# A state-space layer whose scan tables come from DRAM and whose states lie on partition halves

## The chip, the cores and the metric

The kernel runs on one core of a Trainium2 chip. The metric is the device time of one execution in microseconds, as a median of timed runs. The engines are TensorE (PE; PEld is its weight load), VectorE (DVE), ScalarE (ACT), GpSimd (POOL) and SyncE (SP); DMA transfers are issued from SP's, ACT's and POOL's queues.

## The reference

One sequence of 512 tokens with 2048 channels, in float32, passes through a state-space (S5) layer and then a forgetting-attention layer. What matters here is the first: 128 groups of 16 channels, each with 64 complex states.

```python
def s5_ssm(u, a_re, a_im, log_dt, b_re, b_im, c_re, c_im, d_skip):
    """u: (B,S,W) -> Re(C h_t) + D*u_t, h_t = Abar h_{t-1} + Bbar u_t per 16-channel group."""
    ...
    x_re = coef_re * bu_re - coef_im * bu_im
    x_im = coef_re * bu_im + coef_im * bu_re
    ...
    _, _, h_re, h_im = lax.associative_scan(combine, (a_seq_re, a_seq_im, x_re, x_im), axis=1)
    y = (jnp.einsum('bsgp,gcp->bsgc', h_re, c_re.astype(F32))
         - jnp.einsum('bsgp,gcp->bsgc', h_im, c_im.astype(F32)))
    y = y + d_skip.astype(F32).reshape(S5_GROUPS, S5_GROUP) * uf
    return y.reshape(bsz, seq, S5_WIDTH)

def s5_layer(h, g_pre, g_post, w_in, ...):
    xn = rmsnorm(h, g_pre)
    uz = xn @ w_in
    u, z = jnp.split(uz, 2, axis=-1)
    y = s5_ssm(u, a_re, a_im, log_dt, b_re, b_im, c_re, c_im, d_skip)
    y = jax.nn.gelu(y)
    y = y * jax.nn.sigmoid(y @ w_glu.astype(F32) + b_glu.astype(F32))
    y = y.astype(h.dtype) * jax.nn.silu(z)
    return h + rmsnorm(y @ w_out, g_post)
```

## The kernel before

All large products are float32 as three products of split halves (`mm3`, L170 to L172): ACT rounds a weight block `wraw` to `whi` (L84), DVE takes the rest as `wlo` (L151). Phase A (0 to 456 us) holds the 32 projections by `w_in`, 16 blocks of 128 channels of u and 16 of z, each 48 matmuls of 128x512, and the state-space layer in 16 tiles j of 128 channels (8 groups; `NQ` is 4 pairs of groups). Phase B multiplies by `w_glu`, C by `w_out`; then comes attention to 1600 us and the last product. `order_a` lists the steps of phase A: after the start, each tile's `tab`, `ker`, `scan` and `y` stand between projections, so that about three projections go with two tiles. A tile scheduler at build time makes each engine's order from it; the weight loads run on POOL's queue through four `wraw` buffers.

A sequence is cut into 64 chunks of `CL` = 8 tokens. `ssm_params` makes the powers of the decay (`apow`, states on partitions: 64 states of two groups). For each tile, `ssm_tables` builds Bt, powers times the input matrix, on DVE (L72, 128x1024, three operations), turns it by eight PE transposes (`btps`, L424) and copies it to BT by ACT; it also makes the phasors `rot`. `ssm_kernel` builds Et, powers times the output matrix (three operations of 128x1152), multiplies it by `bb` to the taps of a chunk (`kps`, L464), from which DVE and ACT make `ktp`; this goes to DRAM (`kd`, L471) and comes back in eight transfers as the Toeplitz matrix M (L475). `ssm_u` turns u by eight writes to DRAM (`ub`, L485) and one read (U, L487), all on SP. `ssm_scan` takes U times BT (`xps`, L498, real and imaginary apart), rotates it, runs the scan G on DVE (L510) and writes the states before each chunk to `hbd`, a block-diagonal tile in which a pair of groups has 128 columns. `ssm_y` adds two products in `yps`: Et times hbd (L526, 8 matmuls of 128x128), and M times U (L531, 16 of 64x64 on alternating column halves). ACT takes the gelu, and eight writes (`y_d`, L537, SP) store it. z goes to DRAM (`z_d`, L700) on ACT's queue.

The profile counts a float32 matmul as two: the 8 of L526 are 16 rows of the trace, the 16 of L531 are 32; a transpose is one.

Of the kernel before, what the change touches and what calls it, by code (L numbers as in the profile page):

```python
# [1153 lines left out]
```

## Time and profile before

| | |
|---|---|
| three timed runs | 1797.41 us median, 1794.77 to 1800.89 |
| the profiled execution | 1793.25 us, span 1791.5 us |
| granted TensorE clock | 0.998 of full speed (its 2.4 GHz level) |
| PE, DVE, ACT, POOL busy | 1772.2, 1100.7, 588.9, 345.3 us |
| phase A, in which the change lies | 0 to 456 us |

A busy share is an average over phases. In a stage in which PE never pauses, an engine of lower share can still be near its limit; what a step costs is read from its own stretch.

### The profile page before, as it was taken

How to read it: one execution, taken by the hardware profiler on the slowest of the kernel's cores; microseconds unless marked ns; L12 is line 12 of the kernel's file. 1: busy time of each engine (PE TensorE's matmuls, PEld its weight loads, DVE VectorE, ACT ScalarE, POOL GpSimd, SP SyncE). 2: the span in 40 equal slices, each digit the busy share in tenths (PEclk: the TensorE clock that was granted, in tenths of full speed). 3: DMA queues.
4: the chain of work that ended last, by engine and by line, in shares of the span. 5: the costliest groups of instructions: out<-in, count | busy, mean ns of one | idle time of the engine just before them, and what ended most of it. 6: DMA issues, size and time to landing. Idle time of an engine off the chain costs nothing.

```text
span 1791.5 us, 24986 instructions
## 1 busy us (share of the span) xinstructions
PE 1772.2 (99%) x9942; PEld 1504.9 (84%) x9942; DVE 1100.7 (61%) x1598; ACT 588.9 (33%) x977; POOL 345.3 (19%) x241
## 2 busy tenths in 40 slices
PE   9999999999999999999999999999999999999997
PEld 6888888888888888898888888888888888988887
DVE  9789899985765622356664666455654556552235
ACT  7333332322544322225332323232332333332221
POOL 1000000000100000012433433334333343300000
PEclk9999999999999999999999999999999999999999
DMA  9545555545644453343333322232233222235332
GB/s 325 152 136 154 142 153 147 150 144 163 213 148 149 160 190 102 98 135 119 95 89 95 90 94 89 93 99 89 89 93 97 91 96 88 89 118 176 98 113 97
DMA packets 141334, 226.49 MB, mean 126 GB/s; under 512 B 53601, under 2 KB 80497, under 8 KB 140961
## 3 DMA queue, kind: packets, MB, share of 16 engines
q1 hardware_dynamic: 126000, 173.79, 31.4%
q0 software_dynamic: 13056, 47.33, 8.3%
q10 hardware_dynamic: 2160, 3.77, 0.6%
q8 instruction: 78, 1.28, 0.3%
q14 instruction: 40, 0.32, 0.1%
HBM read 201.88 MB, written 22.97 MB: 126 GB/s over the span
## 4 chain that ended last, share of the span: by engine, by line
PE 91%; DVE 4%; DMA 2%; SPq 1%; issue 0%; ACT 0%; DVEq 0%; ACTq 0%
PE proj L170 18%; PE proj L172 18%; PE proj L171 18%; PE tok L230 6%; PE tok L231 6%; PE tok L232 6%; PE v L205 3%; PE v L204 3%; PE v L206 3%; PE yps L526 1%; PE t L938 1%; PE yps L531 1%; PE xps L498 1%; DVE al L75 1%; PE btps L424 1%; DVE wlo L151 1%
## 5 line engine op out<-in xcount | busy, mean ns | idle before, releaser
L151 DVE TENSOR_TENSOR wlo<-wraw,whi 128x1024 fp32r<-128x1024 f32 x284 | 421.9, 1487 | 453.5 <-ACT whi L84 453.4
L84 ACT ACTIVATE whi<-wraw 128x1024 fp32r<-128x1024 f32 (+2 forms) x292 | 305.9, 1049 | 848.8 <-PE proj L172 508.2
L147 POOL TENSOR_TENSOR wraw<-wraw,vecs 128x1024 f32<-128x1024 f32 (+1 forms) x128 | 263.0, 2055 | 622.1 <-DMA wraw<-kv_k 254.8
L170 PE MATMUL proj<-BH,whi 128*128 128x512 f32 (+1 forms) x816 | 309.8, 380 | 0.0
L171 PE MATMUL proj<-BH,wlo 128*128 128x512 f32 (+1 forms) x816 | 307.7, 377 | 2.0 <-DVE wlo L151 2.0
L172 PE MATMUL proj<-BL,whi 128*128 128x512 f32 (+1 forms) x816 | 308.0, 377 | 0.5 <-DVE BL L72 0.5
L170 PE MATMUL proj<-ah,whi 128*128 128x512 f32 x768 | 302.2, 394 | 2.1 <-ACT zt L84 1.8
L171 PE MATMUL proj<-ah,wlo 128*128 128x512 f32 x768 | 299.4, 390 | 0.1
L172 PE MATMUL proj<-al,whi 128*128 128x512 f32 x768 | 299.1, 390 | 0.0
L171 PEld LDWEIGHTS proj<-BH,wlo 128*128 128x128 f32 x816 | 153.6, 188 | 30.2 <-DVE wlo L151 2.4
L172 PEld LDWEIGHTS proj<-BL,whi 128*128 128x128 f32 x816 | 153.5, 188 | 29.3 <-DVE BL L72 0.8
L170 PEld LDWEIGHTS proj<-BH,whi 128*128 128x128 f32 x816 | 153.6, 188 | 27.6
L170 PEld LDWEIGHTS proj<-ah,whi 128*128 128x128 f32 x768 | 144.1, 188 | 33.8 <-ACT zt L84 2.2
L171 PEld LDWEIGHTS proj<-ah,wlo 128*128 128x128 f32 x768 | 144.2, 188 | 30.4 <-DVE wlo L151 0.7
L172 PEld LDWEIGHTS proj<-al,whi 128*128 128x128 f32 x768 | 144.2, 188 | 30.3 <-DVE al L75 0.3
L205 PE MATMUL v<-wlo,BH 128*128 128x512 f32 (+2 forms) x320 | 111.4, 348 | 0.0
L204 PE MATMUL v<-whi,BH 128*128 128x512 f32 (+2 forms) x320 | 111.3, 348 | 0.0
L206 PE MATMUL v<-whi,BL 128*128 128x512 f32 (+2 forms) x320 | 111.3, 348 | 0.0
L230 PE MATMUL tok<-whi,BH 128*128 128x512 f32 (+1 forms) x320 | 111.1, 347 | 0.0
L230 PE MATMUL tok<-whi,ah 128*128 128x512 f32 (+1 forms) x320 | 111.0, 347 | 0.0
L232 PE MATMUL tok<-whi,al 128*128 128x512 f32 (+1 forms) x320 | 110.9, 347 | 0.0
L231 PE MATMUL tok<-wlo,ah 128*128 128x512 f32 (+1 forms) x320 | 110.9, 347 | 0.0
(211 smaller groups left out, 2359.9 us busy)
## 6 DMA issues: line engine op xcount, KB each, us to landing
wraw<-w_fox SPq DMA_DIRECT2D x64, 512.0 KB
wraw<-w_in POOLq DMA_DIRECT2D x58, 512.0 KB, 4.3
wraw<-w_glu POOLq DMA_DIRECT2D x32, 512.0 KB, 4.4
wraw<-w_out SPq DMA_DIRECT2D x32, 512.0 KB
wraw<-kv_k SPq DMA_DIRECT2D x32, 512.0 KB
wraw<-w_fo SPq DMA_DIRECT2D x32, 512.0 KB
wraw<-kv_v SPq DMA_DIRECT2D x28, 512.0 KB
M<-kd SPq DMA_DIRECT2D x128, 64.0 KB
```

The costliest lines, as they stand in the source:

```text
L84: self.nc.scalar.activation(out, in_, f, **kw)
L147: (eng or nc.vector).tensor_tensor(raw, raw, scale.unsqueeze(2).to_broadcast(shp), op=ALU.mult)
L151: (eng if eng and scale is None else nc.vector).tensor_tensor(lo, raw, hi, op=ALU.subtract)
L170: mm(ps, lhsT=hi, rhs=xh, start=(k == 0), stop=False)
L171: mm(ps, lhsT=lo, rhs=xh, start=False, stop=False)
L172: mm(ps, lhsT=hi, rhs=xl, start=False, stop=(k == self.K - 1))
L204: nc.tensor.matmul(o, lhsT=xh[k][:, bs], rhs=hi, start=(k == 0), stop=False)
L205: nc.tensor.matmul(o, lhsT=xh[k][:, bs], rhs=lo, start=False, stop=False)
L206: nc.tensor.matmul(o, lhsT=xl[k][:, bs], rhs=hi, start=False, stop=(k == K - 1))
L230: nc.tensor.matmul(ps, lhsT=xh[k][:, bs], rhs=hi, start=(k == 0), stop=False)
L231: nc.tensor.matmul(ps, lhsT=xh[k][:, bs], rhs=lo, start=False, stop=False)
L232: nc.tensor.matmul(ps, lhsT=xl[k][:, bs], rhs=hi, start=False, stop=(k == K - 1))
```

## The change

- The powers are turned on PE once at the start (`ssm_powers`, new L397, 8 transposes `aps`) and B once for four tiles (`ssm_group`, new L425, 4 transposes `bgps`). Both go to DRAM (`at_d`, `bt_d`). For each tile, `ssm_fetch` reads them back spread over partitions (AT, BTab, 512 KB each, one buffer each, on SP), after the tables of the tile before are made; `ssm_tables` multiplies them to BT directly on DVE. The transposes `btps` and ACT's copies of them are gone.
- Real and imaginary states of a group lie on the two partition halves. H is one tile `hst` of 8 groups by 64 chunks, written by four adds of 64x252 in place of two of 64x504 to `hbd`. The E product (new L563) is 16 matmuls of 64x64, on alternating column halves. Et is 128x1024 from DVE, with its first step of 128x128 copied by ACT; it takes `apow2`, the powers by group, which ACT copies at the start in eight pieces of 64x576.
- u is written in one transfer (`ub`, SP) and read in one. The eight `y_d` writes of a tile and z go on POOL's queue.

```diff
+        self.ts(CO[:, 2, :], CO[:, 1, :], -1.0, ALU.mult)
+        for h in range(2):
+            for c in range(2):
+                nc.sync.dma_start(self.CO2[64 * c:64 * c + 64, :, h], CO[64 * h:64 * h + 64, 0:3 - c:2 - c])
...
+    def ssm_powers(self):
+        nc, sp, A, NG = self.nc, self.sp, self.AP, self.NG
+        for h in range(2):
+            for c in range(2):
+                for x in range(2):
+                    self.act(self.A2[64 * c:64 * c + 64, x, h::2], A[64 * h:64 * h + 64, x])
+        nb = NG // 16
+        for c in range(2):
+            ps = self.bank(name="aps").rearrange("p (b f) -> p b f", f=P)[:, :nb]
+            a = sp.tile([P, nb, CL, 16], F32, tag="B2r", name="at")
+            for b in range(nb):
+                self.act(a[:, b], A[:, c, 16 * b:16 * b + 16, 0:CL].rearrange("p q t -> p t q"))
+                nc.tensor.transpose(ps[:, b], a[:, b].rearrange("p t q -> p (t q)"), self.ident)
+            o = sp.tile([P, nb, P], F32, tag="bsb", name="asb")
+            self.act(o, ps)
+            for b in range(nb):
+                nc.sync.dma_start(self.at_d[b][:, c], o[:, b])
...
+    def ssm_group(self, i, n):
         nc, sp = self.nc, self.sp
-        bc = [P, nq, 32]
-        B4 = self.B4 = sp.tile([P, nq, 3, 16], F32, tag="B4", name="B4")
-        Ca = sp.tile([P, nq, 16, 2], F32, tag="Ca", name="Ca")
-        Cb = sp.tile([P, nq, 16, 2], F32, tag="Cb", name="Cb")
-        self.C4 = [v.rearrange("p q c s -> p q (c s)") for v in (Ca, Cb)]
-        braw = sp.tile([P, nq, 3, 16], F32, tag="braw", name="braw")
-        nc.sync.dma_start(braw[:, :, 1:3], i["ssm_b"][:, q0:q0 + nq])
-        nc.sync.dma_start(Ca, i["ssm_c"][:, q0:q0 + nq])
-        self.act(braw[:, :, 0], braw[:, :, 2], scale=-1.0)
-        co = lambda c: self.CO[:, c, q0:q0 + nq].unsqueeze(2).to_broadcast(bc)
-        two = lambda v, s: v[:, :, s:s + 2].rearrange("p q s c -> p q (s c)")
-        t = sp.tile(bc, F32, tag="tmp", name="gt")
-        self.tt(two(B4, 1), two(braw, 1), co(0), ALU.mult)
-        self.tt(t, two(braw, 0), co(1), ALU.mult)
-        self.tt(two(B4, 1), two(B4, 1), t, ALU.add)
-        self.act(B4[:, :, 0], B4[:, :, 2], scale=-1.0)
-        self.act(Cb, Ca[:, :, :, ::-1], scale=-1.0)
-        self.act(Ca[:, :, :, 1], Ca[:, :, :, 1], scale=-1.0)
+        g0, ng = 32 * n, min(32, 2 * self.NG - 32 * n)
...
+        b1, b2, C1, C2 = (sp.tile([P, ng, 16], F32, tag=t, name=t) for t in ("B1", "B2r", "C1", "C2"))
+        B2 = sp.tile([P, ng // 8, 16, 8], F32, tag="B2", name="B2")
...
+        w = lambda t: t.rearrange("p (b g) c -> p b c g", g=8)
+        self.tt(B2, w(b1), w(b2), ALU.add)
+        self.act(C1[64:], C1[64:], scale=-1.0)
+        ps = self.bank(name="bgps").rearrange("p (b f) -> p b f", f=P)[:, :ng // 8]
+        for b in range(ng // 8):
+            nc.tensor.transpose(ps[:, b], B2[:, b].rearrange("p c g -> p (c g)"), self.ident)
+        o = sp.tile([P, ng // 8, P], F32, tag="bsb", name="bsb")
+        self.act(o, ps)
+        nc.sync.dma_start(self.bt_d[n].rearrange("b r f -> r b f"), o)
+        self.ssm_fetch(4 * n)
+    def ssm_fetch(self, j):
+        nc, sp = self.nc, self.sp
+        AT = sp.tile([P, 2, 8, 64], F32, tag="AT", name="AT")
+        n = 2 * NQ * P
+        s = self.at_d[j // 4]
+        nc.sync.dma_start(AT.rearrange("p c g f -> p (c g f)"),
+                          bass.AP(s.tensor, s.offset + (j % 4) * n, [[0, 16], [4 * n, CL], [1, n]]))
+        BT = sp.tile([P, 8, 2, 64], F32, tag="BTab", name="BTab")
+        s = self.bt_d[j // 4][j % 4]
+        nc.sync.dma_start(BT.rearrange("p g s f -> p (g s f)"),
+                          bass.AP(s.tensor, s.offset, [[8 * P, 16], [0, CL], [1, 8 * P]]))
+        self.tabs = AT, BT
...
-        Bt = sp.tile([P, NQ, 2, 16, CL], F32, tag="Bt", name="Bt")
-        bv = Bt.rearrange("p q s c t -> p q (s c) t")
-        bc = [P, NQ, 32, CL]
-        pw = lambda c: self.AP[:, c, qs, 0:CL].unsqueeze(2).to_broadcast(bc)
-        vv = lambda s: self.B4[:, ql:ql + NQ, s:s + 2].rearrange("p q s c -> p q (s c)").unsqueeze(3).to_broadcast(bc)
-        t = sp.tile(bc, F32, tag="tmp", name="btt")
-        self.tt(bv, pw(0), vv(1), ALU.mult)
-        self.tt(t, pw(1), vv(0), ALU.mult)
-        self.tt(bv, bv, t, ALU.add)
-        BT = T["BT"] = sp.tile([P, NQ, 2, P], F32, tag="BT", name="BT")
-        for q0 in range(0, NQ, 2):
-            bps = self.bank(name="btps").rearrange("p (q c g) -> p q c g", q=2, c=2)
-            for q in range(2):
-                for c in range(2):
-                    nc.tensor.transpose(bps[:, q, c, :], Bt[:, q0 + q, c].rearrange("p c t -> p (c t)"), self.ident)
-            self.act(BT[:, q0:q0 + 2], bps)
+        AT, Bb = self.tabs
+        BT = T["BT"] = sp.tile([P, 8, 2, 64], F32, tag="BT", name="BT")
+        t = sp.tile([P, 8, 2, 64], F32, tag="tmp", name="btt")
+        a = lambda c: AT[:, c].unsqueeze(2).to_broadcast([P, 8, 2, 64])
+        self.tt(BT, a(0), Bb, ALU.mult)
+        self.tt(t, a(1), Bb[:, :, ::-1], ALU.mult)
+        self.tt(BT[:, :, 0], BT[:, :, 0], t[:, :, 0], ALU.subtract)
+        self.tt(BT[:, :, 1], BT[:, :, 1], t[:, :, 1], ALU.add)
+        if j + 1 < self.K and (j + 1) % 4:
+            self.ssm_fetch(j + 1)
...
-        Et = T["E"] = sp.tile([P, NQ, CL + 1, 16, 2], F32, tag="Et", name="Et", bufs=2)
-        ev = Et.rearrange("p q t c s -> p q t (c s)")
-        bc = [P, NQ, CL + 1, 32]
-        pe = lambda c: self.AP[:, c, qs, :].unsqueeze(3).to_broadcast(bc)
-        ve = lambda s: self.C4[s][:, ql:ql + NQ].unsqueeze(2).to_broadcast(bc)
-        t = sp.tile(bc, F32, tag="tmp", name="ett")
-        self.tt(ev, pe(0), ve(0), ALU.mult)
-        self.tt(t, pe(1), ve(1), ALU.mult)
-        self.tt(ev, ev, t, ALU.add)
+        gs = slice(8 * (j % 4), 8 * (j % 4) + 8)
+        B2, C1, C2 = self.gt
+        Et = T["E"] = sp.tile([P, 8, CL + 1, 16], F32, tag="Et", name="Et", bufs=2)
+        t = sp.tile([P, 8, CL, 16], F32, tag="tmp", name="ett")
+        bc = [P, 8, CL, 16]
+        a = lambda c: self.A2[:, c, 8 * j:8 * j + 8, 1:].unsqueeze(3).to_broadcast(bc)
+        c_ = lambda v: v[:, gs].unsqueeze(2).to_broadcast(bc)
+        self.act(Et[:, :, 0], C1[:, gs])
+        self.tt(Et[:, :, 1:], a(0), c_(C1), ALU.mult)
+        self.tt(t, a(1), c_(C2), ALU.mult)
+        self.tt(Et[:, :, 1:], Et[:, :, 1:], t, ALU.subtract)
         bb = self.bb[j % 2]
         for h in range(2):
-            ph = slice(64 * h, 64 * h + 64)
-            self.act(bb[ph, :, :, h, :], self.B4[ph, ql:ql + NQ, 1:3])
+            self.act(bb[:, :, h, h], B2[:, j % 4, :, h::2].rearrange("p c q -> p q c"))
         kps = self.bank(name="kps")[:, :P]
         for q in range(NQ):
-            for c in range(2):
-                nc.tensor.matmul(kps[32 * q:32 * q + 32, :], lhsT=bb[:, q, c].rearrange("p g c -> p (g c)"),
-                                 rhs=Et[:, q, 0:CL, :, c].rearrange("p t c -> p (t c)"),
-                                 start=(c == 0), stop=(c == 1))
+            for h in range(2):
+                nc.tensor.matmul(kps[32 * q:32 * q + 32, :], lhsT=bb[:, q, h].rearrange("p g c -> p (g c)"),
+                                 rhs=Et[:, 2 * q + h, 0:CL].rearrange("p t c -> p (t c)"),
+                                 start=(h == 0), stop=(h == 1))
...
-        self.tt(u.rearrange("p t k -> p k t"), ps.rearrange("p (k t) -> p k t", t=CL),
+        self.tt(u.rearrange("p t k -> p k t")[:, :, ::-1], ps.rearrange("p (k t) -> p k t", t=CL),
                 self.rstd.rearrange("p (k t) -> p k t", t=CL), ALU.mult)
-        ub = self.dp.tile([16, CL, 8, NC], F32, tag="ub", name="ub", bufs=2)
-        for t in range(CL):
-            nc.sync.dma_start(ub[:, CL - 1 - t].rearrange("c g k -> g c k"), u[:, t, :])
+        ub = self.dp.tile([8, 16, CL, NC], F32, name="ub", tag="ub", bufs=2)
+        nc.sync.dma_start(ub.rearrange("g c t k -> (g c) t k"), u)
         U = sp.tile([P, 8, NC], F32, tag="U", name="U", bufs=3)
-        nc.sync.dma_start(U, ub.rearrange("c t g k -> (c t) g k"))
+        nc.sync.dma_start(U, ub.rearrange("g c t k -> (c t) g k"))
...
+        H = self.H.rearrange("p (q h) k -> p q h k", h=2)
         for h in range(2):
             ph = slice(64 * h, 64 * h + 64)
-            self.tt(self.Hbd[ph, :, :, h, 1:], W[ph, :, :, :NC - 1], t[ph, :, :, :NC - 1], ALU.add)
+            for c in range(2):
+                self.tt(H[64 * c:64 * c + 64, :, h, 1:], W[ph, :, c, :NC - 1], t[ph, :, c, :NC - 1], ALU.add)
     def ssm_y(self, j, U, T):
         nc, sp = self.nc, self.sp
         yps = self.bank(name="yps").rearrange("p (g k) -> p g k", k=NC)
-        H, Et, M = self.Hbd, T["E"], T["M"]
-        for q in range(NQ):
-            o = yps[:, 2 * q:2 * q + 2, :].rearrange("p g k -> p (g k)")
-            for c in range(2):
-                nc.tensor.matmul(o, lhsT=Et[:, q, 1:CL + 1, :, c].rearrange("p t c -> p (t c)"),
-                                 rhs=H[:, q, c].rearrange("p g k -> p (g k)"), start=(q == c == 0), stop=False)
+        H, Et, M = self.H, T["E"], T["M"]
+        for g in range(2 * NQ):
+            for h in range(2):
+                nc.tensor.matmul(yps[64 * h:64 * h + 64, g, :],
+                                 lhsT=Et[:, g, 1 + 4 * h:5 + 4 * h].rearrange("p t c -> p (t c)"),
+                                 rhs=H[:, g, :], start=(g == 0), stop=False)
...
-            nc.sync.dma_start(self.y_d[j][g].rearrange("c t k -> t c k"), g_[:, g, :])
+            nc.gpsimd.dma_start(self.y_d[j][g].rearrange("c t k -> t c k"), g_[:, g, :])
...
-                    (nc.sync if n < 2 else nc.scalar).dma_start(self.z_d[j], z)
+                    (nc.sync if n < 2 else nc.gpsimd).dma_start(self.z_d[j], z)
...
                     self.ssm_kernel(j, T[j])
+                    if j + 1 < K and (j + 1) % 4 == 0:
+                        self.ssm_group(i, (j + 1) // 4)
```

On PE, in the steady part of phase A, at the end of a projection; `proj` are its matmuls, and names are those of the section above. Before:

```order
L172 MATMUL proj<-al_270,whi 128x512
L424 MATMUL btps<-ident,Bt 128x128 x8
L526 MATMUL yps<-hbd,Et 128x128 x8
L531 MATMUL yps<-U,M 64x64 x16
L464 MATMUL kps<-Et,bb_129 32x128 x8
L498 MATMUL xps<-U,BT 64x64 x16
L170 MATMUL proj<-ah_149,whi 128x512
```

And now:

```order
L170 MATMUL proj<-ah_225,whi 128x512
L501 MATMUL kps<-Et,bb_140 32x128 x8
L563 MATMUL yps<-hst,Et 64x64 x16
L569 MATMUL yps<-U,M 64x64 x16
L534 MATMUL xps<-U,BT 64x64 x16
L171 MATMUL proj<-ah_225,wlo 128x512
L172 MATMUL proj<-al_226,whi 128x512
```

The transposes are gone, 16 E matmuls of 64x64 stand in the place of 8 of 128x128, and each group of state-space matmuls again stands between projection matmuls.

On PE near the start, at the end of the fourth projection and the beginning of the fifth, before (`ah13` to `al15` are the last rows of x):

```order
L172 MATMUL proj_630<-al13_255,whi_623 128x512
L170 MATMUL proj_630<-ah14_263,whi_623 128x512
L171 MATMUL proj_630<-ah14_263,wlo_624 128x512
L172 MATMUL proj_630<-al14_264,whi_623 128x512
L170 MATMUL proj_630<-ah15_269,whi_623 128x512
L171 MATMUL proj_630<-ah15_269,wlo_624 128x512
L172 MATMUL proj_630<-al15_270,whi_623 128x512
L170 MATMUL proj_708<-ah0_149,whi_681 128x512
```

And now, with the transposes of the powers (`at` is ACT's copy of them):

```order
L172 MATMUL proj_685<-al13_265,whi_678 128x512
L170 MATMUL proj_685<-ah14_273,whi_678 128x512
L171 MATMUL proj_685<-ah14_273,wlo_679 128x512
L397 MATMUL aps_586<-ident_71,at_587 128x128 x3
L172 MATMUL proj_685<-al14_274,whi_678 128x512
L397 MATMUL aps_586<-ident_71,at_587 128x128
L170 MATMUL proj_685<-ah15_279,whi_678 128x512
L171 MATMUL proj_685<-ah15_279,wlo_679 128x512
L172 MATMUL proj_685<-al15_280,whi_678 128x512
L170 MATMUL proj_763<-ah0_159,whi_736 128x512
L397 MATMUL aps_602<-ident_71,at_603 128x128
L171 MATMUL proj_763<-ah0_159,wlo_737 128x512
```

The first three transposes stand after the 44 first matmuls of the fourth projection, the second four among the first matmuls of the fifth, whose first ones they now precede.

On POOL's queue, before, from its first transfer to the end of phase B's loads:

```order
L557 DMA ident<-c_ident 128x128
L559 DMA eye_73<-c_eye 128x16
L855 DMA mask<-c_mask 128x128
L145 DMA wraw<-w_in 128x1024 x58
L145 DMA wraw<-w_glu 128x1024 x32
```

And now, for two tiles in the steady part (`gy` is the gelu's output):

```order
L744 DMA z_d_101<-zt 128x512
L145 DMA wraw<-w_in 128x1024
L575 DMA y_d_84<-gy 8x16x64 x8
L145 DMA wraw<-w_in 128x1024 x2
L575 DMA y_d_85<-gy 8x16x64 x8
L145 DMA wraw<-w_in 128x1024 x3
L744 DMA z_d_102<-zt 128x512
L145 DMA wraw<-w_in 128x1024
L575 DMA y_d_86<-gy 8x16x64 x8
```

Each tile's eight y writes and a z now stand between weight loads in one queue.

## Rows read from the trace of the kernel before

**Rows 1.** The page: the span, the busy time of each engine (share of the span, count of instructions), and the shares of the chain that ended last, by engine.

```profile
span 1791.5 us, 24986 instructions
...
PE 1772.2 (99%) x9942; PEld 1504.9 (84%) x9942; DVE 1100.7 (61%) x1598; ACT 588.9 (33%) x977; POOL 345.3 (19%) x241
...
PE 91%; DVE 4%; DMA 2%; SPq 1%; issue 0%; ACT 0%; DVEq 0%; ACTq 0%
```

**Rows 2.** The chain that ended last, from 116 to 165 us: start, duration, engine, name, line; "x16" joins consecutive instructions of a line.

```profile
118.24 0.93 PE xps L498 x32
...
119.83 0.23 PE proj L172
...
130.28 0.87 PE btps L424 x8
131.15 1.88 PE yps L526 x16
133.03 1.08 PE yps L531 x32
...
146.97 0.87 PE btps L424 x8
...
159.35 2.08 PE yps L526 x16
161.44 1.08 PE yps L531 x32
```

**Rows 3.** Busy time by stretch of five pairs of tiles: start and end; length, then of each engine its busy microseconds and (x) its instructions, the granted clock, the DMA engines' mean busy share, GB/s.

```profile
core 0: us, PE busy (x) PEld busy (x) DVE busy (x) ACT busy (x) POOL busy (x), PEclk, DMA share, GB/s
...
118.24:162.52 44.28, 44.28 (x358) 37.30 (x356) 41.34 (x48) 15.20 (x28) 3.18 (x6) 1.00 0.56 152
162.52:206.80 44.28, 44.28 (x358) 37.32 (x356) 39.55 (x45) 13.62 (x23) 3.18 (x6) 1.00 0.52 146
206.80:251.05 44.25, 44.25 (x358) 37.32 (x356) 39.76 (x47) 14.47 (x25) 2.65 (x5) 1.00 0.54 145
251.05:295.33 44.28, 44.28 (x359) 37.31 (x356) 40.94 (x46) 14.12 (x25) 3.71 (x7) 1.00 0.54 153
295.33:339.61 44.28, 44.28 (x358) 37.31 (x356) 41.37 (x48) 14.77 (x26) 3.18 (x6) 1.00 0.52 145
```

**Rows 4.** The instructions on the tile `btps` on PE: minimum, median and maximum duration in ns, first and last start.

```profile
L424 PE MATMUL btps<-ident,Bt x128: 271/272/273, 88.2 to 413.2; 128*128 128x128 f32 x128
```

**Rows 5.** DVE's costliest groups from 115 to 385 us by form: names, shapes, count; busy us, mean ns of one; idle time of DVE just before them and who ended most of it.

```profile
L151 DVE TENSOR_TENSOR wlo<-wraw,whi 128x1024 fp32r<-128x1024 f32 x37 | 45.1, 1220 | 3.7 <-ACT whi L84 3.6
L72 DVE TENSOR_TENSOR Et<-apow,Ca 128x1152 f32<-128x1152 f32 x13 | 17.6, 1354 | 1.9 <-PE yps L526 1.9
...
L72 DVE TENSOR_TENSOR hbd<-hw,ht 64x504 f32<-64x504 f32 x24 | 16.3, 678 | 0.6
L72 DVE TENSOR_TENSOR ett<-apow,Cb 128x1152 f32<-128x1152 f32 x12 | 16.3, 1355 | 0.2
...
L72 DVE TENSOR_TENSOR btt<-apow,B 128x1024 f32<-128x1024 f32 x12 | 14.7, 1222 | 0.2
L72 DVE TENSOR_TENSOR Bt<-Bt,btt 128x1024 f32<-128x1024 f32 x12 | 14.6, 1221 | 0.2
...
L72 DVE TENSOR_TENSOR zt<-rot,xps 128x512 f32<-128x512 f32 x13 | 8.9, 684 | 4.0 <-PE xps L498 4.0
...
L75 DVE SCALAR_TENSOR_TENSOR ktp<-eye,vecs,kps 128x16 f32<-128x16 f32 x13 | 3.0, 227 | 14.2 <-PE kps L464 14.2
```

**Rows 6.** PE in order of time, the first matmul of the fourth projection: start, duration; in brackets the idle time before it and who ended it.

```profile
43.16 0.50 PE L170 MATMUL proj<-ah,whi 128*128 128x512 f32 x1 [1.80 <-ACT zt L84]
```

**Rows 7.** DVE in order of time at the last step of the powers (`apow`): start, duration, line. L121 is the first product, L123 writes the real parts, L126 the imaginary ones.

```profile
48.31 0.42 DVE L121 TENSOR_TENSOR scr<-apow 128x256 f32<-128x256 f32 x1
...
49.37 0.42 DVE L123 TENSOR_TENSOR apow<-scr 128x256 f32<-128x256 f32 x1
...
51.00 0.48 DVE L126 TENSOR_TENSOR apow<-scr 128x256 f32<-128x256 f32 x1
```

**Rows 8.** ACT in order of time over the same stretch: start, duration.

```profile
43.02 0.42 ACT L84 ACTIVATE phasors<-scr 128x128 f32<-128x128 f32 x1
...
48.09 0.62 ACT L84 ACTIVATE dec<-rdec 128x504 f32<-128x504 f32 x1
...
49.12 1.04 ACT L84 ACTIVATE whi<-wraw 128x1024 fp32r<-128x1024 f32 x1
```

**Rows 9.** The weight loads issued by POOL (L145), over the whole run: minimum, median and maximum ns of an issue, and the time from issue to landing.

```profile
L145 POOL DMA_DIRECT2D wraw<-w_in x58: 530/530/536, 20.9 to 416.1; - x58
...
DMA to landing us min/median/max: 3.8/4.3/8.0
```

**Rows 10.** The waits of SP's queue from 115 to 385 us: line, what it waited for, total us, times, longest.

```profile
SPq L475 <- DMA kd<-ktp: 25.3, 13, 3.2
SPq L471 <- ACT ktp L84: 22.1, 7, 4.9
```

**Rows 11.** The waits of PE from 0 to 460 us, of the y matmuls: total us, times, longest.

```profile
PE yps L531 <- DMA M<-kd: 1.0, 2, 0.8
```

More of the change, by code (lines that the diff above doesn't have):

```diff
@@ L311, in ssm_params @@
         A, E, R, CO = self.AP, self.E, self.R, self.CO
-        s1 = sp.tile([P, 16, NG], F32, tag="Bt", name="scr1")
+        s1 = sp.tile([P, 16, NG], F32, tag="AT", name="scr1")
         s2 = sp.tile([P, 17, NG], F32, tag="tmp", name="scr2")
@@ L360, in ssm_params @@
         self.tt(R, t, t, ALU.mult)
-        c, si = E[:, :, :, 1], E[:, :, :, 2]
+        c, si = E[:, :, 0:4:3], E[:, :, 1:5:3]
         nc.vector.memset(c[:, :, :, 0], 1.0)
@@ new lines, in ssm_params @@
+        self.ts(E[:, :, 2], E[:, :, 4], -1.0, ALU.mult)
+        self.ssm_powers()
+    def ssm_powers(self):
[15 more added lines that the diff above has]
+                nc.sync.dma_start(self.at_d[b][:, c], o[:, b])
@@ new lines, in ssm_group @@
+    def ssm_group(self, i, n):
+        nc, sp = self.nc, self.sp
+        g0, ng = 32 * n, min(32, 2 * self.NG - 32 * n)
+        gs = slice(g0, g0 + ng)
+        b1, b2, C1, C2 = (sp.tile([P, ng, 16], F32, tag=t, name=t) for t in ("B1", "B2r", "C1", "C2"))
+        B2 = sp.tile([P, ng // 8, 16, 8], F32, tag="B2", name="B2")
+        self.gt = B2, C1, C2
+        for x in range(2):
+            nc.sync.dma_start((b1, b2)[x], i["ssm_b"][x][:, gs])
+            nc.sync.dma_start((C1, C2)[x], i["ssm_c"][x][:, gs])
+        co = lambda x: self.CO2[:, x, :, g0 // 2:(g0 + ng) // 2].rearrange("p h q -> p q h").unsqueeze(3).to_broadcast(
+            [P, ng // 2, 2, 16])
+        v = lambda t: t.rearrange("p (q h) c -> p q h c", h=2)
+        self.tt(v(b1), v(b1), co(0), ALU.mult)
+        self.tt(v(b2), v(b2), co(1), ALU.mult)
+        w = lambda t: t.rearrange("p (b g) c -> p b c g", g=8)
[8 more added lines that the diff above has]
+        self.ssm_fetch(4 * n)
@@ L497, in ssm_scan @@
                     pg = slice(64 * g, 64 * g + 64)
-                    nc.tensor.matmul(X[pg, q, c], lhsT=T["BT"][:, q, c, pg], rhs=U[:, 2 * q + g, :],
+                    nc.tensor.matmul(X[pg, q, c], lhsT=T["BT"][:, 2 * q + g, c], rhs=U[:, 2 * q + g, :],
                                      start=True, stop=True)
@@ L607, in phase_a @@
             sp = self.sp = ctx.enter_context(tc.tile_pool(name="ssm", bufs=1))
-            self.AP = sp.tile([P, 2, self.NG, CL + 1], F32, name="apow")
-            self.E = sp.tile([P, self.NG, 2, 3, 8], F32, name="phasors")
+            self.AP = sp.tile([P, 2, self.NG, CL + 1], F32, tag="Et", name="apow", bufs=2)
+            self.A2 = sp.tile([P, 2, 2 * self.NG, CL + 1], F32, name="apow2")
+            self.CO2 = sp.tile([P, 2, 2, self.NG], F32, name="coef2")
+            self.E = sp.tile([P, self.NG, 5, 8], F32, name="phasors")
+            nb = self.NG // 16
+            self.at_d = [self.dp.tile([CL * 4, 2, NQ, P], F32, name=f"at_d{b}") for b in range(nb)]
+            self.bt_d = [self.dp.tile([4, P, P], F32, name=f"bt_d{n}") for n in range(nb)]
             self.R = sp.tile([P, self.NG], F32, name="rdec")
@@ L628, in phase_a @@
             self.ktp = [sp.tile([P, 240], F32, name=f"ktp{b}") for b in range(2)]
-            self.Hbd = sp.tile([P, NQ, 2, 2, NC], F32, name="hbd")
-            for t in self.dec + self.bb + self.ktp + [self.Hbd]:
+            self.H = sp.tile([P, 8, NC], F32, name="hst")
+            for t in self.dec + self.bb + self.ktp + [self.H]:
                 nc.vector.memset(t, 0.0)
@@ L699, in phase_a @@
                     self.act(z, ps)
-                    (nc.sync if n < 2 else nc.scalar).dma_start(self.z_d[j], z)
+                    (nc.sync if n < 2 else nc.gpsimd).dma_start(self.z_d[j], z)
                 elif c == "u":
                     if j == 0:
-                        self.rows(rstd, self.rstd, sp, "gt")
+                        self.rows(rstd, self.rstd, sp, "rt2")
                     U[j] = self.ssm_u(j, ps)
@@ L1128, in layouts, with halves @@
     a["ssm_a"] = c(np.stack([st(g["s5_a_re"][0]), st(g["s5_a_im"][0]), st(ld)], 1))
-    a["ssm_b"] = c(np.stack([g[n][0].reshape(NG, P, 16).transpose(1, 0, 2) for n in ("s5_b_re", "s5_b_im")], 2))
-    a["ssm_c"] = c(np.stack([g[n][0].reshape(NG, 2, 16, 64).transpose(1, 3, 0, 2).reshape(P, NG, 16)
-                             for n in ("s5_c_re", "s5_c_im")], 3))
+    def halves(re, im):
+        return c(np.stack([np.concatenate(v, 0) for v in ((re, im), (im, re))]))
+    a["ssm_b"] = halves(*(g[n][0].transpose(1, 0, 2) for n in ("s5_b_re", "s5_b_im")))
+    a["ssm_c"] = halves(*(g[n][0].transpose(2, 0, 1) for n in ("s5_c_re", "s5_c_im")))
     a["c_ident"] = np.eye(P, dtype=np.float32)
```

19 lines of the change are left out of this document (7 added, 12 removed).

## The prediction

> **What bounds the kernel now.** I read the busy shares first: TensorE (PE) is busy 1772.2 of 1791.5 us and 91% of the chain that ended last is PE, so only less work on PE, or a new gap in it, can move the time [rows 1]. All that the change touches lies in phase A, the first 456 us, so I read that stage by itself. Between 118 and 340 us it repeats every 44.28 us, and in each such stretch PE has no idle time at all [rows 3]. The chain there shows what fills it: three projections of 48 matmuls at 0.23 us, and the state-space matmuls of two tiles j [rows 2]. VectorE (DVE) matters as much for what comes next: in the same stretches it is busy 39.6 to 41.4 us, 40.6 on average [rows 3]. PE has only 3.7 us per pair of tiles to lose before DVE is the longer one.
>
> **What it takes off PE.** The eight `btps` transposes take 0.87 us of the chain per tile, 0.109 each [rows 2]; a matmul's own duration, 271 ns, overlaps its neighbours' and isn't the price [rows 4]. The E product (L526) takes 1.88 and 2.08 us in the two tiles of a pair [rows 2]. After, its 16 matmuls a tile of 64 columns by 64 on alternating column halves have the shape, the weights and the pattern of the 16 of L531, which the profile counts as 32 and which take 1.08 us [rows 2]. I take 1.08 us; the ends are 0.93, the `xps` group with as many matmuls of that size, and 1.98, the mean of the form it replaces. A pair then saves 2 x 0.87 + 3.96 - 2.16 = 3.54 us. Every fourth tile gets four transposes `bgps` of 0.109, 0.22 a pair. Net 3.32 us a pair: 44.28 becomes 40.96, and eight pairs give 26.6 us.
>
> **What DVE can follow.** Removed per tile: three Bt operations of 1.22, three Et operations of 1.36, two hbd adds of 0.68, together 9.10 us [rows 5]. Added: two BT products of 128x1024 (1.22 each) and two halves of 128x512 (0.69 each, the price of zt), three Et operations of 128x1024 (1.22 each), four hst adds of 64x252. Of those the trace has no row; by elements per lane the nearest is the 128x256 operation at 0.42 [rows 7], the dearest bound is the 0.68 of hbd [rows 5]. At 0.42 the sum is 3.82 + 3.66 + 1.68 = 9.16: DVE gains nothing. Its 40.6 us a pair now stand against 40.96 of PE, and DVE also waits: 14.2 us before ktp, 4.0 before zt, 3.7 before wlo and 1.9 before Et over some twelve tiles, 4.0 a pair [rows 5]. These are waits for PE or for ScalarE (ACT) at places where DVE's own order has nothing ready. A part is slack that shrinks when PE comes sooner; a part is latency that stays. With none left the pair is 40.96, with all left 40.6 + 4.0, which is no gain. The `kps` row stands behind most of it, and the new order gives DVE two or three other operations between `Et` and `ktp`; I keep 1.0 us a pair. The forecast is 41.6 us, a gain of 2.7 a pair and **21.4 us** over eight. What is late next is `kps` on PE, waiting for Et, and the y matmuls, waiting for hst.
>
> **The start.** Eight transposes `aps` stand in PE's order before the last projection matmuls of the fourth and between the first of the fifth. PE starts the fourth projection at 43.16 [rows 6] and reaches the first after some 44 matmuls of 0.23, at 53.4. They read copies by ACT that wait for the powers: real parts complete at 49.79, imaginary ones at 51.48 [rows 7]. ACT then has eight copies of 64x576 ahead of them (0.62 by the 128x504 row, nearly 0.55 back to back), one whi (1.04) and four copies of 128x128 (0.42, or 0.34 back to back) [rows 8]: 49.8 + 4.4 + 0.95 + 1.3 = 56.5 for the fourth. PE loses about 3.1 us there. The second set follows after an evacuation (0.6), a copy and another whi, at 59 to 59.5, where PE stands about half a microsecond earlier: 0.5. With the transposes themselves (0.87), less about 1.0 of the 1.8 us that PE waits at 43.16 for zt now, since fewer of ACT's copies stand ahead of that zt, **+3.4**. If the scheduled copies start late, this is +6; if ACT finds the whi not yet landed and passes none, it can't go below +1.5. The first tile's tables come through DRAM: a write and a read, some 2 and 4.3 us by the kd and weight rows [rows 9, 10]. 75 projection matmuls (17 us) stand between `bgps` and the first `xps`, which covers it but for the build; I put **+0.6**.
>
> **The fetched tables.** Two reads of 512 KB a tile are added, on SyncE's (SP) queue. Reads of that size land 4.3 us after issue (3.8 to 8.0) [rows 9]. AT has one buffer: it is fetched again once tile j's two products have read it, and is needed about a period later (20.8 us), less 3.8 of build. Two of them at the slow end, 16 us, still fit. The share of the DMA engines, 0.52 to 0.56 [rows 3], rises by 1 MB in 20.8 us, 48 GB/s on some 150, less what the shorter u write saves. I cost it at nothing; the cover is that slack of some 17 us, and without it each late microsecond costs one per tile, 15 in all.
>
> **The queues.** SP goes from 26 issues a tile to 13. It is not late in the steady stretch: its largest waits are for data, not behind other issues [rows 10]. Where it is late is the end: PE waits 1.0 us at L531 for M [rows 11]; I book **-1.0**. The y writes (8 a tile) and z go behind the weight loads on GpSimd's (POOL) queue. An issue there takes 0.53 us, at most 0.536, with DVE over 90% busy beside it [rows 9, 3]. 8 of y, 3 of weights and about 1 of z make 12 x 0.53 = 6.4 us in a period of 20.8. The weight load waits behind y issues that wait for a gelu, but it stands some two projections ahead of its use. Cost nothing. The Trainium skill's page "SBUF — State Buffer" (section "SBUF: two separate sides", the "DVE blocks DMA" trap) speaks against this move: a transfer issued by GpSimd has its descriptors written by GpSimd's cores, which are locked out while DVE runs a two-port operation, and 620 ns become some 3100 ns; by it an estimate of 12 issues is 37 us, more than the period. The 58 weight issues at 530 to 536 ns show none of it against this kernel's DVE operations.
>
> **The end of phase A.** In the new order only about 40 and 33 projection matmuls (9.2 and 7.6 us) stand between the last tiles' steps, where DVE's chain for a tile needs more, and kps, ktp, kd and M take another 7 to 10 us of issue and landing; I put **+1.5** (0 to +5). Phases B to E run the same instructions.
>
> **Sum.** -21.4 + 3.4 + 0.6 - 1.0 + 1.5 = -16.9; I round to -16, since every unknown but the E product ends on the dear side. The profiled run took 1793.25, 4.2 under the median of 1797.41 and 1.5 under the fastest of the three timed runs (1794.77 to 1800.89); from it 1777, from the median **1781 us**, which I predict.
>
> **Rivals.** (a) DVE keeps up and PE's whole gain stays: pairs of 40.96 or, with the E product at 0.93, 40.66; -26.6 + 3.4 + 0.6 - 1.0 = -23.6 with nothing lost at the end, **1774**; with 2.4 from the E product and half of the start's loss, 1769. For it: DVE's busy sum is below PE's. Against: by 0.4 us in 41, with waits in a fixed order.
> (b) DVE's waits don't shrink: 40.6 + 4.0 is a pair as long as now, less a half microsecond a pair; -4 + 3.4 + 0.6 + 1.5 - 1.0 = 0, **1797**. For it: ktp waits 14.2 us though PE is never idle. If hst costs 0.68 an add, DVE has 2.1 us a pair more and it becomes **1814**, slower.
> (c) The other side, by POOL: if each issue had to wait for the DVE operation under way (1.22 us), 12 x 1.75 = 21.0 us fill the period; two operations each make 12 x 2.97 = 35.6, 13.5 more than today's 22.1, and with 16 tiles 215 us, **2012**. It decides from 1.85 us per issue. Against it: the 0.536 at most of [rows 9].
> (d) The first set of `aps` or the tail costs double: -21.4 + 7 + 1 + 5 - 1 = -9, **1788**, still faster.
>
> **How the numbers follow.** The forecast with (d), 1773 to 1790: 0.52. (a): 0.20. (b): 0.22, of which 0.07 slower. (c) and a late fetch: 0.06, mostly slower. Measurement tells 0.3%, 5.4 us, from no change. Faster (below 1792): 0.52 + 0.20 + 0.03 of (b); same: 0.13; slower: 0.12. The range takes in (a) and, of (b), what is no slower, 1768 to 1798; the slower cases stay outside. The likeliest's own range is 1773 to 1790.
>
> **What would show it.** Right: the pair's period 41 to 42 us; the 16 E matmuls at 0.9 to 1.2 us; PE idle for the first time in the steady stretch, about 0.6 us a pair, before kps or the E product and released by DVE; a gap of about 3 us near 53 us, released by ACT; POOL issues at 0.53. Wrong: PE idle before xps released by a DMA (fetch late); POOL issues above 1 us; 16 E matmuls taking near 2 us, or DVE adds hst at 0.68.

## The result, and the profile after

The changed kernel is slower: 1818.96 us (1816.43 to 1820.19, 4 runs) against 1798.63 (1794.77 to 1800.89, 4 runs), a ratio of 1.0113, interval 1.0091 to 1.0136. I had forecast 1781. PE has less to do, and for the first time it pauses all through phase A; the page, with the rows that answer to [rows 1]:

```profile
span 1818.4 us, 25317 instructions
...
PE 1768.4 (97%) x10094; PEld 1490.2 (82%) x10094; DVE 1109.7 (61%) x1647; ACT 584.3 (32%) x971; POOL 429.6 (24%) x382
...
PE 74%; DVE 13%; DMA 8%; issue 2%; SPq 1%; ACT 1%; POOL 0%; DVEq 0%; ACTq 0%
```

In the chain that ended last VectorE rose from 4% to 13% and the transfers from 2% to 8%. Four of the waits of PE up to 490 us (total us, times, longest):

```profile
PE kps L501 <- DVE Et L72: 16.0, 14, 2.7
PE yps L563 <- DVE hst L72: 5.7, 4, 2.3
PE yps L569 <- DMA M<-kd: 4.1, 5, 1.2
PE aps L397 <- ACT at L84: 3.0, 1, 3.0
```

And four of the waits of VectorE from 60 to 460 us. None of them had a counterpart before, where no wait of VectorE in that stretch was for a transfer:

```profile
DVE B2r L72 <- DMA B2r<-ssm_b: 10.2, 3, 5.4
DVE BT L72 <- DMA BTab<-bt_d: 9.2, 2, 5.8
DVE btt L72 <- DMA BTab<-bt_d: 8.8, 6, 3.2
...
DVE B L72 <- DMA B<-ssm_b: 2.1, 1, 2.1
```

Together 30.3 us of waiting for B and for BTab. The state-space run, from the first `kps` to the last, is no shorter: first the changed kernel, then the one before (duration ns; first and last start in us).

```profile
L501 PE MATMUL kps<-Et,bb x256: 269/273/423, 116.8 to 446.0; 128*32 128x128 f32 x128
```

```profile
L464 PE MATMUL kps<-Et,bb x256: 273/282/313, 89.2 to 418.7; 128*32 128x128 f32 x128
```

It takes 329 us in both, but begins 27.6 us later. The stretch of that run, with the columns of [rows 3], after and then before:

```profile
117.00:447.00 330.00, 306.63 (x2730) 248.92 (x2726) 289.24 (x377) 89.59 (x158) 97.64 (x168) 0.96 0.70 193
```

```profile
90.00:419.00 329.00, 327.98 (x2620) 275.78 (x2622) 297.66 (x336) 106.34 (x183) 23.85 (x45) 1.00 0.53 147
```

PE was busy 21 us less, 13 of them because 59 fewer projection matmuls stand in the stretch (0.227 each); 74 more stand ahead of it. Its idle time rose from 1 to 23 us, its mean clock fell to 0.96, and the DMA engines' share rose from 0.53 to 0.70. Phase A ends 24.6 us later (480.5 against 455.9, the start of the first matmul of the phase behind it); 2.3 us are added after it, which no step here explains. The two profiled executions lie 26.9 us apart and the medians 20.3, as the profiled run before was shorter than all its timed ones; stretches of the two profiles are compared here, not times.

### The profile page after: what moved, and what is told of

The parts are those of the page before. It is cut to its first block, busy times and chain, and to the rows that moved or that the text cites. A ratio compares the mean times of both kernels' runs of the same rounds, so it can differ in the third digit from the quotient of the medians.

```text
span 1818.4 us, 25317 instructions
## 1 busy us (share of the span) xinstructions
PE 1768.4 (97%) x10094; PEld 1490.2 (82%) x10094; DVE 1109.7 (61%) x1647; ACT 584.3 (32%) x971; POOL 429.6 (24%) x382
## 4 chain that ended last, share of the span: by engine, by line
PE 74%; DVE 13%; DMA 8%; issue 2%; SPq 1%; ACT 1%; POOL 0%; DVEq 0%; ACTq 0%
PE proj L170 13%; PE proj L172 13%; PE proj L171 13%; PE tok L231 6%; PE tok L230 6%; PE tok L232 6%; PE v L205 3%; PE v L204 3%; PE v L206 3%; DVE wlo L151 2%; DMA BTab<-bt_d 2%; DMA M<-kd 1%; DVE BT L72 1%; PE t L984 1%; DMA B2r<-ssm_b 1%
## 5 line engine op out<-in xcount | busy, mean ns | idle before, releaser
L151 DVE TENSOR_TENSOR wlo<-wraw,whi 128x1024 fp32r<-128x1024 f32 x284 | 405.8, 1430 | 461.4 <-ACT whi L84 458.0
L147 POOL TENSOR_TENSOR wraw<-wraw,vecs 128x1024 f32<-128x1024 f32 (+1 forms) x128 | 269.4, 2105 | 621.1 <-DMA wraw<-kv_k 256.5
```

The costliest lines, as they stand in the source:

```text
L147: (eng or nc.vector).tensor_tensor(raw, raw, scale.unsqueeze(2).to_broadcast(shp), op=ALU.mult)
L151: (eng if eng and scale is None else nc.vector).tensor_tensor(lo, raw, hi, op=ALU.subtract)
```

## The experiments

Times are medians, ratios are to the kernel before on the same chip, with intervals; the last columns are the starts of the first and the last `kps` in the profile.

| kernel | us | ratio | first | last |
|---|---|---|---|---|
| changed | 1819.0 | 1.0113 (1.0091 to 1.0136) | 116.8 | 446.0 |
| e1 first group early | 1812.6 | 1.0088 (1.0070 to 1.0105) | 102.1 | 443.8 |
| e9 later groups two tiles ahead | 1804.6 | 1.0036 (1.0020 to 1.0052) | 116.6 | 432.5 |
| e5 both | 1795.4 | 0.9994 (0.9982 to 1.0005) | 99.1 | 420.7 |
| e11 both, no tables in 12 tiles | 1780.9 | 0.9914 (0.9897 to 0.9931) | 97.3 | 404.5 |
| e2 no tables in 12 tiles | 1797.0 | 1.0003 (0.9992 to 1.0015) | 115.7 | 416.9 |
| e7 no fetch in 12 tiles | 1811.2 | 1.0083 (1.0062 to 1.0103) | 116.2 | 437.1 |
| e10 as e5, fetch on ACT | 1797.3 | 1.0006 (0.9991 to 1.0020) | 100.6 | 427.6 |
| e12 as e5, rot on GpSimd | 1813.1 | 1.0095 (1.0079 to 1.0110) | 106.3 | 437.6 |
| e4 y, z queues back | 1820.6 | 1.0138 (1.0115 to 1.0161) | 116.5 | 449.1 |
| e3 halves alone | 1797.0 | 1.0005 (0.9993 to 1.0016) | 89.9 | 416.5 |
| e8 transfers alone | 1795.3 | 0.9988 (0.9976 to 1.0001) | 89.6 | 416.8 |
| **e6 halves and transfers** | **1779.9** | **0.9910 (0.9893 to 0.9926)** | 90.1 | 403.0 |

**Is it the late start?** e1:

```diff
-        if j == 0:
-            self.ssm_group(i, 0)
...
                 if n == 0:
                     self.ssm_params(i)
+                    self.ssm_group(i, 0)
```

> The changed kernel, with the first group's tables begun right after the powers, ahead of the two u projections, not at the first tile's own step. Late-start theory: the changed kernel's first kps stands at 116.8 us (89.2 before), and after it VectorE sets the pace, so the 25 us are never made up; here the first kps comes back to 90 to 95 us and the time falls by 15 to 25 us, to 1794 to 1804. Steady-pace rival (the pace of a tile, 21.3 us, and the low clock after each gap are what costs, the start only moves projections about): at most 5 us better than 1819.

The first `kps` came back to 102.1, 14.7 us earlier, and 6 us of the time came back with it (4.5 by the ratios). The late-start theory as I stated it fell, and its rival, at most 5, is the nearer one: the run from the first to the last `kps` took longer (342 us), with PE waiting for Et:

```profile
PE kps L499 <- DVE Et L72: 24.1, 7, 6.5
```

**Is it the tables?** e2 skips the fetch and, but for each four's first tile, the four operations that make BT.

> The changed kernel without the table fetch and the four VectorE operations that build BT in 12 of the 16 tiles (it reuses the first tile's of each four; its output is not the reference's). If VectorE, with its own work and its waits for the tables, is the bound from the first tile on: its work falls by 12 x 3.8 = 46 us and most of the 18 us of waits go, PE becomes the bound again, and the time falls by 25 to 40 us, to 1780 to 1794, with a clock near 1.00 in the steady stretch. If PE's own lateness (late start, queue order) is the cause: less than 12 us.

22 us better, 3 short of the least that was expected: as much as the whole loss. It takes away VectorE's work on the tables and its waits for them together, so it does not tell the two apart. With its first `kps` at 115.7 the kernel still does no better than the one before.

**Which part of the change holds?** e3 puts the halves alone on the kernel before (Et, `hst` and the E product as in the diff, `bb` from the old table by four copies), e4 takes the queues back in the changed kernel, e8 has the transfers alone, e6 the halves and the transfers.

> The kernel before with one part of the change alone: real and imaginary states on partition halves, so the E product is 16 matmuls of 64 by 64; tables by transposes, u and the y and z writes stay as before. PE loses 0.9 us a tile, 14.4 in all, VectorE 0.1 a tile, and nothing is put ahead of the first tile but ACT's eight copies. If PE's gain is real as long as VectorE isn't made later: 1784 to 1790. If VectorE cannot follow any faster PE: 1794 to 1799.

> The changed kernel with y written on SyncE's queue and z on ScalarE's, as before. If the writes on GpSimd's queue cost (0.594 us an issue, late weight loads): 5 us or more better than 1819. If they are hidden: within 3 us of 1819, or a little slower, since the table fetches then stand behind eight more issues a tile on SyncE's queue (8 x 0.62 = 5 us a tile).

> The kernel before with the halves and the transfers (u in one write, y and z on GpSimd's queue), but with the tables by transposes. In the run with the halves alone PE waited 7.3 us for M behind a full SyncE queue, 6 of them at the last tiles, and a pair of tiles took 42.9 us in place of 44.28. If SyncE's queue held the rest of the gain: those waits go and the time is 1784 to 1790. If the writes on GpSimd's queue or VectorE's pace hold it: 1793 to 1799.

> The kernel before with the transfers alone (u in one write, y and z on GpSimd's queue). PE waits for SyncE's queue only 1.0 us in phase A there, so 1795 to 1798 if nothing else depends on it. If 0.594 us an issue on GpSimd, or a u write that takes 4.5 us to land in place of eight small ones, delays weights or U: 1800 or more.

e3 gained nothing in time, but not for VectorE's sake: to the fifteenth tile it was 8 us ahead (`xps` at 392.3 against 400.3), and lost 6 at the last, behind SP's queue:

```profile
PE yps L536 <- DMA M<-kd: 7.3, 6, 3.9
```

e8 shows that the transfers alone are worth nothing, e4 that taking back the queues of y and z gains nothing in the changed kernel, and e6 that together with the halves the transfers are worth 17 us. SP is not late until PE is faster: PE's waits for M fall from 7.3 us in e3 to 2.0 in e6, and five pairs of tiles, from the fourth on, take 211.0 us in place of 216.9. e6 beats both kernels, and the best that I expected of it by 4 us. PE's wait for M in e6:

```profile
PE yps L535 <- DMA M<-kd: 2.0, 2, 1.2
```

Its chain shows the E product (L529) at the price that I had given it, 1.08 for 32:

```profile
214.27 0.87 PE btps L426 x8
215.14 1.08 PE yps L529 x32
216.22 0.93 PE yps L535 x32
```

Undoing the tables in the changed kernel, which is what e6 is, gives back 37 us by the ratios, 39 by the medians.

**Where do the tables cost it?** e7 leaves out the fetch and keeps the work; e9 turns each later group's B two tiles ahead (B2 in two buffers, C loaded where it was); e5 has e9 and e1.

```diff
-                    if j + 1 < K and (j + 1) % 4 == 0:
-                        self.ssm_group(i, (j + 1) // 4)
+                    if j + 1 < K and (j + 1) % 4 == 0:
+                        self.ssm_group_c(i, (j + 1) // 4)
+                    if j + 3 < K and (j + 3) % 4 == 0:
+                        self.ssm_group(i, (j + 3) // 4)
```

> The changed kernel with the first group's tables begun early (as in the run that did that alone) and every later group's B turned and written to DRAM two tiles ahead of its use, its scaled B in two buffers; C is loaded where it was, and the fetch for a group's first tile goes out with the others, a tile ahead. In the changed kernel VectorE waited 12.3 us for loads of B and 18.0 us for BTab in phase A, in the main at the groups' beginnings. Late-transfer theory: those 30 us of waits, and PE's idle time and low clock behind them, go: 1790 to 1800. Rival (VectorE and PE in a fixed order with no slack, whatever arrives when): no better than 1808.

> The changed kernel without the table fetch of 12 tiles (it builds BT each time from the tables of each four's first tile; its output is not the reference's). VectorE's work is the same as in the changed kernel. If the fetch of each tile (1 MB, its place on SyncE's queue, its traffic) costs: half or more of the 22 us that leaving out fetch and build together gave, 1800 to 1808. If it is the build's 3.8 us a tile on VectorE and the groups' beginnings: within 5 us of 1819.

> The changed kernel with each later group's B turned two tiles ahead, but with the first group where the changed kernel has it. Beginning the first group early gave 6 us alone, and both together 24 us. If the two are separate causes that add: about 17 us better than 1819, 1800 to 1804. If they work only together (the late start leaves VectorE the pace-maker in either case): less than 8 us better.

The later groups' beginnings alone are worth 14 us (e9) and the start alone 6 (e1); together they are worth 24 (e5), the start 9 of them. So the causes add, to within 3 us; e9 itself stayed 3 short of the 17 that I expected. One group's beginning in the changed kernel, SP's queue and then VectorE in order of time:

```profile
268.35 0.37 SPq L428 DMA_DIRECT2D bt_d<-bsb  x1
272.25 5.50 SPq L512 DMA_DIRECT2D M<-kd  x8
277.80 0.60 SPq L442 DMA_DIRECT2D BTab<-bt_d  x1
```

```profile
276.37 1.72 DVE L72 TENSOR_TENSOR hst<-hw,ht 64x252 f32<-64x252 f32 x4
283.92 1.23 DVE L72 TENSOR_TENSOR BT<-AT,BTab 128x1024 f32<-128x1024 f32 x1 [5.83 <-DMA BTab<-bt_d]
```

The write of bt_d is issued at 268.4 (the four such writes land 3.0 to 6.4 us after issue), but its read stands behind the landing of kd and eight issues of M, goes out at 277.8 and lands at 283.9; VectorE has nothing else in its order, and waits 5.8 us. e7, which builds BT of all tiles from the tables of each four's first, gives 5 us by the ratios, 8 by the medians, between its two theories: the fetch of the other tiles costs something, but less than half of what fetch and build together cost.

**What holds e5 back?** e10 moves the fetch to ACT's queue (`nc.sync` to `nc.scalar` in `ssm_fetch`); e11 is e5 without tables, like e2; e12 gives the three operations of `rot` to GpSimd.

> The run with the early first group and the others two tiles ahead, with the two table fetches of a tile issued on ScalarE's queue in place of SyncE's, where they stood behind kd's landing and eight issues of M. VectorE waited 15.3 us for BTab in that run. If these waits were what kept it from falling below the kernel before: 1783 to 1790. If VectorE's own 42 us a pair are the pace: within 3 us of 1795.

> The run with the early first group and the others two tiles ahead, without the fetch and the building of BT in 12 of the 16 tiles (it reuses the BT of each four's first; its output is not the reference's). It settles what holds that run at 1795 although PE has 11 us less work than in the run with halves and transfers alone (1780). If VectorE's pace: its work falls by 46 us, PE is the bound, and with 11 us less work than at 1780, but some 10 lost at the start, the time is 1775 to 1783. If the start or SyncE's queue hold it: 1789 or more.

> The run with the early first group and the others two tiles ahead, with the three operations that make rot (128x512) on GpSimd in place of VectorE. VectorE has 2.1 us a tile less, 33 us in all. If VectorE's pace is the bound and GpSimd's operations stay off the path: 1780 to 1788, perhaps the level of the run with halves and transfers alone. If GpSimd is late with them (some 1 us each at the 2.06 us per 1024 columns of the attention phase, behind table waits in its queue) or slows VectorE beside it: 1793 or more.

In e10 VectorE no longer waits for BTab, yet the time is the same. In e5 the profile puts 11.2 us down to BTab, not 15.3; for 4.1 more before the same operation it names no one. First e5, then e10:

```profile
DVE btt L72 <- DMA BTab<-bt_d: 11.2, 8, 3.1
...
DVE ktp L75 <- PE kps L507: 7.6, 7, 2.4
...
DVE btt L72 <- issue: 4.1, 1, 4.1
```

```profile
DVE ktp L75 <- PE kps L507: 21.5, 11, 3.7
```

The waits for `kps` took their place, 14 us more of them. e11, with 36 us less of busy time on VectorE in phase A (347.7 against 383.7 in e5), comes down to e6. So what is left of e5's loss goes with the building and the fetching of the tables. As e10 gains nothing without the waits for BTab, VectorE's work and its order are the likelier part, but no run takes away the one and keeps the other. One pair of the steady part in e5, e6 and e11:

```profile
258.00:300.00 42.00, 40.48 (x350) 33.04 (x346) 37.69 (x50) 11.25 (x19) 12.67 (x22) 1.00 0.73 202
```

```profile
258.00:300.00 42.00, 42.00 (x388) 35.17 (x386) 40.05 (x50) 14.48 (x30) 13.46 (x23) 1.00 0.54 155
```

```profile
258.00:300.00 42.00, 41.27 (x374) 33.91 (x373) 34.92 (x48) 12.53 (x23) 13.49 (x23) 1.00 0.62 172
```

Five pairs from the fourth tile on (starts of `xps`) take 210.8 us in e5, 211.0 in e6 and 206.3 in e11. PE is full in e6; in e5 it has less to do and the pair is as long. The 15 us between e5 and e6 lie ahead of that: 9 before the first `kps`, 6 over the first three tiles, where B came late once more. e12 was a miss of its own kind: an operation that takes VectorE 0.69 us takes GpSimd 1.8 to 2.9, and VectorE's hst rose from 0.41 to 0.59 beside it (us, then the mean in ns).

```profile
L476 POOL TENSOR_TENSOR rot<-phasors 128x512 f32<-128x512 f32 x12 | 34.9, 2908 | 24.9 <-DVE hw L72 24.9
L477 POOL TENSOR_TENSOR rt<-phasors 128x512 f32<-128x512 f32 x12 | 25.1, 2093 | 8.2 <-DVE hst L72 8.2
L478 POOL TENSOR_TENSOR rot<-rot,rt 128x512 f32<-128x512 f32 x12 | 21.2, 1766 | 0.9
...
```

```profile
L72 DVE TENSOR_TENSOR hst<-hw,ht 64x252 f32<-64x252 f32 x48 | 28.5, 593 | 0.6
```

## Why the prediction was wrong

The forecast was 38 us too low. By the runs, 14 of them are the later groups' beginnings (changed to e9), 9 the start (e9 to e5), and 14.5 the building and fetching of the tables in the other tiles (e5 to e11). That e11 then stands at the forecast, 1780.9, is in part luck: its first `kps` is 8.1 us late, where 4.0 were forecast for the start, and its pair takes 41.3 us in place of 41.6.

- **PE's savings: right.** The E product took 1.08 us a tile (in e6), the transposes went, `aps` cost its wait of 3.0 us (3.1 forecast).
- **VectorE's sum: right.** It was busy 388.7 us of phase A before and 384.6 after. hst took 414 ns and the halves of BT 679 (0.42 and 0.69 forecast), from 115 to 385 us by form:

```profile
L72 DVE TENSOR_TENSOR hst<-hw,ht 64x252 f32<-64x252 f32 x48 | 19.9, 414 | 0.7
L72 DVE TENSOR_TENSOR BT<-BT,btt 128x512 f32<-128x512 f32 x24 | 16.1, 679 | 0.0
```

- **The pace, 41.6 us a pair: too low as a term.** Over the same five pairs it is 45.9 in the changed kernel (229.7 us), no shorter than before (44.28); 43.3 in e9 (216.4) and 42.2 in e5, whose groups begin in time. So VectorE's waits did not shrink, which is rival (b)'s case (44.6), though its waits were now for transfers. At 42.2 the transposes' removal is worth nothing, since e6, which keeps them, has the same pair.
- **The first tile, +0.6: the step that failed first.** I said that 75 projection matmuls "cover" the tables' way through DRAM. They cover it on PE, but they are taken from the tiles behind, and the state-space run starts 27.6 us later: 17.0 for these 75 matmuls, 7.2 by which the matmuls ahead of them were already late (3.4 forecast), and 3.4 of pauses right before the first `kps`. Behind it the pace is set by VectorE and the transfers that it waits for, and the run is no shorter. A first `kps` at 99.1 in place of 116.6 gave 9 us (e9 to e5).
- **The groups' beginning: a step that I left out.** I priced `bgps` at 0.109 a transpose and the fetches "at nothing", with a cover of 17 us a tile. That cover exists for three tiles of four; for each four's first tile B's load, its scaling, the turn, the write and the read stand one behind the other, in SP's queue among kd and M. It cost 14 us (e9), and 30 us of VectorE's waits. The sign that I had named for a late fetch, PE idle before `xps` behind a transfer, did not come: the lateness stood on VectorE and reached PE as waits for Et and hst. The reads were also slower than [rows 9]: 6.6 us for AT and 8.0 for BTab (last column, median us from issue to landing) where the weights had 4.3 before, and 5.0 in the changed kernel:

```profile
AT<-at_d SPq DMA_DIRECT2D x16, 512.0 KB, 6.6
BTab<-bt_d SPq DMA_DIRECT2D x16, 512.0 KB, 8.0
```

- **The queues: right alone, wrong in company.** The transfers are worth nothing by themselves (e8), 17 us beside the halves (e3 to e6). Rival (c), GpSimd, did not come: the 128 y issues took 0.594 us, at most 0.643. The trap on the Trainium skill's page "SBUF — State Buffer" (section "SBUF: two separate sides"), which is for a VectorE operation in a two-port mode, shows in none of them.
- **The clock: not in the sum.** PE's matmuls took some 17.5 us longer at the lower clock; see below.

What stays open: how the 14.5 us between e5 and e11 divide between VectorE's 3.8 us of building a tile and the late transfers that go with it. By the starts of `xps`, e11 gains 1.8 us ahead of the first tile, 6.2 over the next three tiles and 4.5 over the five pairs, so most of it isn't the steady pace. Each variant also has its own order of instructions from the scheduler, and no run holds that order fixed.

## What to carry to other kernels

Where two engines are both over 90% busy, work taken off one is worth only the other's slack, and a new wait on either can cost time, though not always its length (here 14 us behind the groups' beginnings, nothing behind e5's waits for BTab): price the change by the fixed order of both, and follow every new transfer from the first instruction that makes its data, through its queue, to the one that reads it, at the group where there is nothing to hide it. Work moved ahead of a chain's start is not hidden by it; it shifts the chain, and what that costs has to be measured (an earlier start by 14.7 us gave 6 alone). And test the parts of a change apart and together: here two parts gave nothing alone, 0.9% together, and the third took more than both gave.
